# Turning attention weights by DMA: one read instead of four, and more of the query tiles turned that way

## The chip, the cores and the metric

The kernel runs on one core of a Trainium2 chip. The metric is the device time of one execution in microseconds (us), and a kernel's time is the median of its runs. A profile is taken of one execution; its span is the time between the first and the last instruction that the profiler records.

The engines are PE (TensorE, matmuls and transposes through the array; its weight loads are listed apart as PEld), DVE (VectorE), ACT (ScalarE), POOL (GpSimd) and SP (SyncE, which here only issues DMAs). Each works through its own instructions in the order in which they were emitted.

## The reference

One layer of a hybrid trunk, in float32, for a prompt of 1024 rows and a sample group of 32 rows: an RMS norm, one projection to eight parts (q, k, v, g for the head groups A and B), attention in 8 heads of 64 in each group, gates, an output projection, and a gated addition of a second embedding. Only the attention matters here:

```python
def band_attention(q, k, v, q_pos, k_pos, bias_table):          # group A
    s = jnp.einsum('bqhd,bkhd->bhqk', q, k).astype(jnp.float32) * ATTN_SCALE
    s = s + bias_table[:, rel].astype(jnp.float32)[None]
    ...
    w = jax.nn.softmax(s, axis=-1).astype(v.dtype)
    return jnp.einsum('bhqk,bkhd->bqhd', w, v)

def stick_breaking(q, k, v, q_pos, k_pos):                      # group B
    z = jnp.einsum('bqhd,bkhd->bhqk', q, k).astype(jnp.float32) * ATTN_SCALE
    ...
    w = jnp.where(causal, jnp.exp(log_beta + after), 0.0).astype(v.dtype)
    return jnp.einsum('bhqk,bkhd->bqhd', w, v)
```

In A, a query row sees its own chunk of 64 and the eight chunks before; in B it sees all rows before it. The weights `w` have a query row in each partition when they are made, and the product with `v` needs a key in each partition: every tile of weights has to be turned.

## The kernel before, in words

All calls go to a `Recorder` (it stands for `nc`), which notes each instruction with what it reads and writes. At the end a planner (`plan`, line 418, with `due` for due times) runs through all of them with a cost for each, and so settles the order on every engine; `emit` writes the instructions out in that order. In the profile they all have one line, L494, that of `emit`; groups are told apart by the names of their tiles. For PE the order follows a class and the place in the recording: attention has class 0 and is taken when its inputs are ready by the plan, projections have class 1 and fill the rest. All DMAs are issued from SP.

Attention goes by eight pairs of heads, A0, B0, A1, B1 and so on, two heads in each pair. While a pair's attention runs, the projections k, q and v of the next pair (tiles `mm_kA` and so on) are woven in; the last pair has the eight gate projections beside it. A head has eight tiles of 128 query rows, i = 0 to 7. Tile i covers `cost(i)` blocks of 128 keys: in A i + 1 up to 5, in B i + 1 up to 8. For each tile there are two steps:

- `scores(i)`: q times k into PSUM (`SA`, `SB`, each with a high part and a low part of k, `kdA` and `klA`), then, in SBUF, the unnormalised weights. Two tiles are used: `om` (from `ring0`, 3076 columns), which takes the biased scores or the running product, and `be` (from `ring1`, 3328 columns), which takes the weights, by an exponential on ACT in A and by a difference on POOL in B. `rooms(i)` hands out both; the rings are used again from the start when they are full, and a place waits for the last use of what lay there.
- `weights_t(i)`: the turn. It makes `wTh` (a copy of the turned weights, rounded to PE's format) and `wTl` (what the rounding left), one 128x128 block for each block of keys.

The step `values(g)` multiplies them with v for the tiles 0 to 3 (g = 0) and 4 to 7 (g = 1), into `PVA` or `PVB`; it needs the turns of all its tiles. Two tiles lie between the scores of a tile and its turn in the recording (`LAG_T = 2`).

There are two ways to turn a tile. Tiles that do not stand in `ROUND` are turned on PE: a transpose for each block into PSUM (`ptwA`, `ptwB`), up to four blocks in one bank, a copy of the bank by ACT to `wTh`, and a subtraction by DVE that reads the bank and `wTh` and writes `wTl`. Tiles in `ROUND` (4 and 6 of A and of B) go by DMA: DVE transposes all 32x32 squares of `be` into `om` (STREAM_TRANSPOSE `om<-be`), SP issues a write of `om` to a scratch tensor in DRAM (`swapA<-om`, `swapB<-om`), and four reads, each to 32 partitions of `be` (`be<-swapA`, `be<-swapB`), put the squares where they belong. ACT then copies the whole tile to `wTh`, and DVE subtracts from SBUF to get `wTl`. There are four reads because square c of a block holds the columns 32c to 32c + 31, which become the partitions 32c to 32c + 31: each read serves the 32 partitions of one c.

The same way is used for the columns of v in `values_out` (`turn`, once for each of the 8 pairs): `vxA<-stvA` by DVE, a write to `swapA`, four reads into `stvA`; ACT then copies `vtA<-stvA`. The keys (`ktA`, `ktB`) are transposed by DVE alone and written straight out.

Of the kernel before, what the change touches and what calls it, by code (L numbers as in the profile page):

```python
# [13 lines left out]
P = 128  # L14
D = 1024
SEQ = 1024
# [11 lines left out]

ROUND = {"A": ((4,),(6,)), "B": ((4,),(6,))}
LAG_T = 2
LAG_V = 2
SPACE_S = 0.1
# [8 lines left out]
def f(ap):  # L43

    return ap.bitcast(F32)
# [454 lines left out]
def stream_step(  # L500
# [7 lines left out]
    nc = rec  # L508
    dma = nc.sync.dma_start
# [10 lines left out]
    def scratch(shape, name):  # L520
        return Buf(shape, F32, name=name, real=dram.tile(shape, F32, tag=name, name=name))
# [3 lines left out]
    og_dr = scratch([8, P, T], "og_dr")  # L525
    h1_dr = scratch([T, D], "h1_dr")
    sum_dr = {w: scratch([4, 4, P, 512], f"sum_dr{w}") for w in "og"}
    r_dr = scratch([8, 768], "r_dr")
    vs_dr = {ab: scratch([NS, 512], f"vs_dr{ab}") for ab in "AB"}
    ple_dr = scratch([T, D], "ple_dr")  # L530

# [83 lines left out]
    def load_x(t):  # L615
        n = min(P, T - t * P)
        if t == 3:
            x34.append(at.tile([P, ringh.cols], F32, tag="wTh", name="x34")[:, 0:2 * D].rearrange("p (a c) -> p a c", a=2))
        xt = x34[0][:, t - 3] if t in (3, 4) else ring0.tile([P, D], f"x{t}")
        dma(xt[0:n], x_prompt[0, t * P:t * P + n, :] if t < 8 else x_sample[0])  # L620
# [8 lines left out]
    def scale_x(t, xt, n, gp):  # L629
        sq = ring1.tile([P, D], f"sq{t}")  # L630
        ms = small.tile([P, 1], F32, tag="ms", name=f"ms{t}", bufs=4)
        nc.scalar.activation(sq[0:n], xt[0:n], AF.Square, scale=1.0 / 32.0, accum_out=ms[0:n])
        r = rstd_of(ms, f"rs{t}", n)
        for kh in range(2):
            nc.vector.scalar_tensor_tensor(sq[0:n, HALF[kh]], xt[0:n, HALF[kh]], r[0:n], gp[kh][0:n], ALU.mult, ALU.mult)
        return sq
# [68 lines left out]
    def short_block(src, out, nm):  # L705
        pt = psum("T", nm)
        nc.tensor.transpose(pt[0:NS, 0:P], src[:, SEQ:T], ident)
        nc.scalar.copy(out[0:NS, 8, :], pt[0:NS, 0:P])
# [19 lines left out]
    def values_out(ab, p, src, o_p, o_s, then):  # L728

        h2 = slice(2 * p, 2 * p + 2)  # L730
        b0 = 4 if ab == "A" else 0
        box = {}

        def turn():
            st = src()
            D = scratch([P, SEQ], f"swap{ab}{p}")
            x = at2.tile([P, SEQ], F32, tag="tok", name=f"vx{ab}{p}", bufs=2)
            nc.vector.transpose(x.rearrange("p (c b f) -> p b c f", c=4, f=32), st[:, 0:SEQ])
            dma(D, x)
            for c in range(4):  # L740
                part = D[:, c * 256:(c + 1) * 256].rearrange("(g t) x -> t g x", t=32)
                dma(st[32 * c:32 * c + 32, 0:SEQ].rearrange("t (g x) -> t g x", g=4), part)
            out = at2.tile([P, NT, P], F32, tag="tok", name=f"vt{ab}{p}", bufs=2)
            box["out"] = out
            short_block(st, out, f"ptv{ab}{p}")

        def back():
            out = box["out"]
            nc.scalar.copy(out[:, 0:8, :].rearrange("p b (g f) -> p g b f", g=4), src()[:, 0:SEQ].rearrange("p (g b f) -> p g b f", g=4, f=32))
            dma(o_p[0, 0, :, h2, :].rearrange("(b p) h d -> p b (h d)", p=P), out[:, b0:8, :])  # L750
            dma(o_s[0, 0, :, h2, :].rearrange("p h d -> p (h d)"), out[0:NS, 8, :])
            then(out)

        return [(0.1, turn), (0.0, back)]
# [79 lines left out]
    def attention(ab, p, h):  # L834

        nm = f"{ab}{p}{h}"
# [12 lines left out]
        def lo_block(i):  # L849
            return max(0, i - 4) if ab == "A" else 0  # L850

        together = {i: g for g in ROUND[ab] for i in g}
        whole, done_with = {}, []

        def cost(i):
            return i + 1 - lo_block(i)
# [63 lines left out]
        def weights_t(i):  # L920
            g = i // 4
            step, size = LAID[ab, g]
            if g not in wT:
                wT[g] = [x.tile([P, size * P], f"{x.name}{nm}_{g}") for x in (ringh, ringl)]
            b0 = lo_block(i)
            w0, w1 = state.pop(i)
            n = i + 1 - b0
            at_ = ((i - 4 * g) * step + b0) * P
            hi, lo = (x[:, at_:at_ + n * P] for x in wT[g])
            if i in together:  # L930

                group = together[i]
                done_with.append((i, hi, lo))
                if i != group[-1]:
                    return
                w0, w1 = whole[group]
                m = sum(cost(x) for x in group)
                first = {x: sum(cost(y) for y in group[:k]) for k, x in enumerate(group)}
                squares = w0[:, 0:m * P].rearrange("p (c b q) -> p b c q", c=4, q=32)
                for x, _, _ in done_with:  # L940
                    y = slice(first[x], first[x] + cost(x))
                    nc.vector.transpose(squares[:, y], w1[:, y.start * P:y.stop * P])
                dr = scratch([P, m * P], f"swap{nm}_{i}")
                dma(dr, w0[:, 0:m * P])
                for c in range(4):
                    x = dr[:, c * m * 32:(c + 1) * m * 32].rearrange("(g k) x -> k g x", k=32)
                    dma(w1[32 * c:32 * c + 32].rearrange("k (g x) -> k g x", g=4), x)
                turned = w1.rearrange("p (g b q) -> p g b q", g=4, q=32)
                for x, hi, lo in done_with:
                    src = turned[:, :, first[x]:first[x] + cost(x), :]  # L950
                    hi, lo = (y.rearrange("p (b g q) -> p g b q", g=4, q=32) for y in (hi, lo))
                    nc.scalar.copy(hi, src)
                    nc.vector.tensor_tensor(lo, src, f(hi), ALU.subtract)
                done_with.clear()
                return
            for b in range(0, n, 4):
                m = min(4, n - b)
                pt = psum("T", f"ptw{nm}_{i}_{b}")
                for x in range(m):
                    nc.tensor.transpose(pt[:, x * P:(x + 1) * P], w1[:, (b + x) * P:(b + x + 1) * P], ident)  # L960
                c = slice(b * P, (b + m) * P)
                nc.scalar.copy(hi[:, c], pt[:, 0:m * P])
                nc.vector.tensor_tensor(lo[:, c], pt[:, 0:m * P], f(hi[:, c]), ALU.subtract)
# [284 lines left out]
    for n in range(-1, 8):  # L1248
        a = len(order)
        if n < 7:  # L1250
            ab, p = pairs[n + 1]
# [503 lines left out]
    for m, (nm, src, group) in enumerate(sets):  # L1755
        last_set = m == len(sets) - 1
        state = [{}, {}]
        for n, prod in enumerate(ORDER):
            for pair, t in enumerate(group):
                st = state[pair]  # L1760
# [28 lines left out]
                b = blocks[nm, WHICH[prod]]  # L1789
# [70 lines left out]
        if m in (0, 2):  # L1860
            if m == 0:
                row = Row(8, fb.tile([P, D], F32, tag="GP", name="h1_8"))
                row.load()
                for q in range(2):
                    y = short_product(nm, short, q)
# [3 lines left out]
            else:  # L1869
                for q in range(2):  # L1870
                    g8 = Gate(8, HALF[q])
                    y = short_product(nm, short, q)
# [38 lines left out]
```

## Time and profile before

| | |
|---|---|
| runs | 797.0, 799.42, 802.35 us; median 799.42 |
| profiled execution | 796.26 us |
| its span | 794.2 us |
| attention stage, about | 62 to 572 us |
| mean granted clock of TensorE | 0.999 of full speed |
| DMA in all | 161.08 MB, 67.4% of 16 engines' span on the queue that SP issues to |

How to read it: the page gives for each engine its busy time and its share of the span, and forty slices of the span with a digit for the busy tenths in each. The chain is followed back from the last instruction, at each step to what released it. A group of instructions has a line with the output and the input tile, the shapes, the count, the busy time of the group, the mean of one in ns, and the idle time of the engine ahead of them with what ended it. In the list of waits a line has the total, the number of times and the longest, in us. In the chain in order of time a line has the start, the length and what it was; pieces follow one another without overlap.

### The profile page before, as it was taken

The page shows a single profiled execution, that of the slowest core. Times are in us where ns is not written, and L with a number is a line of the kernel's source. Part 1 is how long each engine was busy: PE and PEld are TensorE (multiplying, and loading weights), DVE is VectorE, ACT ScalarE, POOL GpSimd, SP SyncE. Part 2 cuts the span into 40 slices and gives each one's busy share as a digit, 9 for nine tenths or more (in the row PEclk, how much of TensorE's full clock was granted, in tenths as well). Part 3 has the DMA queues.
Part 4 walks back from the last instruction along what each step waited for, and adds up shares of the span by engine and source line. Part 5 has one row for each costly group of instructions (what it writes and reads, how often), then busy time and mean ns, then how long its engine had stood idle before and what let it go on. Part 6 is the DMA issues. An engine that isn't in the chain of part 4 may idle for free.

```text
span 794.2 us, 14262 instructions
## 1 busy us (share of the span) xinstructions
PE 781.9 (98%) x4646; PEld 723.1 (91%) x4646; DVE 572.6 (72%) x1007; ACT 503.8 (63%) x1061; POOL 438.9 (55%) x503
## 2 busy tenths in 40 slices
PE   9999989999999999999999999999999999999997
PEld 7999989999999999999999999999997877888786
DVE  6716868887688889877878788883354878676655
ACT  5636765767686548874677586532348967875741
POOL 5624546874547675424670436787544358597613
PEclk9999999999999999999999999999999999999999
DMA  8519987668887759744544776756489847668634
GB/s 264 170 42 289 229 246 206 180 183 234 233 256 225 206 164 280 194 135 159 132 118 148 169 208 189 234 177 190 126 269 332 282 138 267 225 222 301 232 126 133
DMA packets 160971, 161.08 MB, mean 203 GB/s; under 512 B 39153, under 2 KB 120793, under 8 KB 160898
## 3 DMA queue, kind: packets, MB, share of 16 engines
q1 hardware_dynamic: 160898, 160.18, 67.4%
q8 instruction: 37, 0.61, 0.3%
q14 instruction: 36, 0.29, 0.1%
HBM read 99.23 MB, written 52.49 MB: 191 GB/s over the span
## 4 chain that ended last, share of the span: by engine, by line
PE 91%; DMA 2%; DVE 2%; POOL 2%; issue 1%; ACT 1%; SPq 1%; DVEq 0%; ACTq 0%; POOLq 0%
PE mm_gB L494 6%; PE mm_gA L494 6%; PE mm_qB L494 6%; PE mm_kB L494 6%; PE mm_vA L494 5%; PE mm_kA L494 5%; PE mm_vB L494 5%; PE mm_qA L494 5%; PE PVB L494 4%; PE SB L494 4%; PE SA L494 4%; PE PVA L494 4%; PE ptwB L494 3%; PE g0P L494 2%; PE g1P L494 2%; PE o1P L494 2%
## 5 line engine op out<-in xcount | busy, mean ns | idle before, releaser
L494 POOL TENSOR_TENSOR be<-om 128x384 f32<-128x384 f32 (+7 forms) x64 | 79.0, 1241 | 64.7 <-DVE om L494 38.8
L494 DVE TENSOR_TENSOR_SCAN om<-om,SB 128x384 f32<-128x384 f32 (+5 forms) x96 | 94.2, 999 | 8.7 <-ACT om L494 7.6
L494 ACT ACTIVATE om<-SB 128x384 f32<-128x384 f32 (+5 forms) x96 | 44.4, 492 | 34.0 <-DVE SB L494 23.0
L494 ACT ACTIVATE be<-om,statA 128x640 f32<-128x640 f32 (+4 forms) x64 | 44.5, 696 | 10.1 <-DVE statA L494 6.5
L494 ACT CAST wTh<-ptwB 128x512 fp32r<-128x512 f32 (+3 forms) x64 | 29.4, 481 | 19.5 <-PE ptwB L494 12.2
L494 DVE TENSOR_TENSOR wTl<-ptwB,wTh 128x512 fp32r<-128x512 f32 (+3 forms) x64 | 34.0, 547 | 10.4 <-ACT wTh L494 7.4
L494 DVE TENSOR_TENSOR wTl<-be,wTh 128x640 fp32r<-128x640 f32 (+1 forms) x32 | 35.3, 1105 | 4.7 <-ACT wTh L494 4.3
L494 DVE TENSOR_TENSOR wTl<-ptwA,wTh 128x512 fp32r<-128x512 f32 (+2 forms) x64 | 30.3, 483 | 10.3 <-ACT wTh L494 9.0
L494 DVE CUSTOM_DVE_ANT_0 om<-SA,biasA 128x320 f32<-128x320 f32 (+2 forms) x64 | 29.7, 483 | 9.0 <-PE SA L494 8.3
L494 ACT CAST wTh<-ptwA 128x512 fp32r<-128x512 f32 (+2 forms) x64 | 26.1, 424 | 13.3 <-PE ptwA L494 11.5
L494 DVE STREAM_TRANSPOSE om<-be 128x640 f32<-128x640 f32 (+1 forms) x32 | 29.0, 906 | 6.1 <-POOL be L494 3.5
L494 PE MATMUL SB<-klB,LB 128*128 128x384 f32 (+5 forms) x96 | 33.0, 348 | 0.0
L494 PE MATMUL SB<-kdB,LB 128*128 128x384 f32 (+5 forms) x96 | 32.9, 347 | 0.1
L494 POOL TENSOR_TENSOR oB<-oB,oB 128x256 f32<-128x256 f32 x32 | 24.2, 777 | 13.8 <-DMA oB<-in_w_out_dram 12.5
L494 DVE TENSOR_TENSOR SB<-SB,maskb 128x128 f32<-128x128 f32 x64 | 17.7, 292 | 19.1 <-PE SB L494 19.0
L494 PE MATMUL SA<-klA,LA 128*128 128x320 f32 (+2 forms) x96 | 29.4, 319 | 1.1 <-DMA klA<-klA 1.1
L494 PE MATMUL SA<-kdA,LA 128*128 128x320 f32 (+2 forms) x96 | 30.0, 323 | 0.0
L494 POOL TENSOR_TENSOR gB<-gB,gB 128x256 f32<-128x256 f32 x32 | 26.0, 832 | 6.8 <-DMA gB<-in_w_ple_gate_dram 6.7
L494 PE MATMUL ptwA<-ident,be 128*128 128x128 f32 x160 | 26.2, 273 | 2.7 <-ACT sumrowA L494 2.7
L494 ACT CAST wTh<-be 128x640 fp32r<-128x640 f32 (+1 forms) x32 | 25.0, 781 | 6.1 <-DMA be<-swapA 4.1
L494 PE MATMUL ptwB<-ident,be 128*128 128x128 f32 x192 | 28.7, 273 | 0.0
L494 POOL TENSOR_TENSOR sggA<-sggA,oggA 128x352 f32<-128x352 f32 x24 | 24.9, 1038 | 5.2 <-DMA be<-swapB 2.9
(707 smaller groups left out, 2655.0 us busy)
## 6 DMA issues: line engine op xcount, KB each, us to landing
swapA<-om SPq DMA_DIRECT2D x16, 320.0 KB, 3.6
be<-swapA SPq DMA_DIRECT2D x64, 80.0 KB, 2.8
oB<-in_w_out_dram SPq DMA_DIRECT2D x16, 256.0 KB
sum_dro<-oB SPq DMA_DIRECT2D x16, 256.0 KB, 4.3
gB<-in_w_ple_gate_dram SPq DMA_DIRECT2D x16, 256.0 KB, 4.2
sum_drg<-gB SPq DMA_DIRECT2D x16, 256.0 KB, 2.6
x<-in_x_prompt_dram SPq DMA_DIRECT2D x16, 256.0 KB, 4.1
h_dr<-h SPq DMA_DIRECT2D x8, 512.0 KB, 4.2
```

The lines of the kernel that those rows point to most:

```text
L494: getattr(getattr(tc.nc, o.what[0]), o.what[1])(*args, **kw)
```

## The change

Two edits go together.

The squares that DVE transposes are no longer made of 32 neighbouring columns, but of every fourth column: square c of a block has the columns c, c + 4, c + 8 and so on up to c + 124. After the transpose, the partition 32g + k of `om` holds, for each c, what belongs into the partition 4k + c. Laid out in DRAM as four parts of 128 rows, where row 4k + c of part g is the piece for partition 4k + c, the write is the same as before, and a single read gives each of the 128 partitions its four pieces, one from each part. Four reads of 32 partitions become one of 128; the bytes and the length of a contiguous piece (m x 32 elements, 640 bytes for five blocks) are the same. The input of the DVE transpose is now read with a step of four elements (16 bytes). The value columns get the same edit.

`ROUND` now lists, each by itself, the tiles 4, 5, 6 and 7 of A and 4, 5 and 6 of B. So tiles 5 and 7 of each A head, and tile 5 of each B head, go by DMA and no longer over PE.

```diff
-ROUND = {"A": ((4,),(6,)), "B": ((4,),(6,))}
+ROUND = {"A": ((4,),(5,),(6,),(7,)), "B": ((4,),(5,),(6,))}
...
         def turn():
             st = src()
-            D = scratch([P, SEQ], f"swap{ab}{p}")
+            D = scratch([4, P, SEQ // 4], f"swap{ab}{p}")
             x = at2.tile([P, SEQ], F32, tag="tok", name=f"vx{ab}{p}", bufs=2)
-            nc.vector.transpose(x.rearrange("p (c b f) -> p b c f", c=4, f=32), st[:, 0:SEQ])
-            dma(D, x)
-            for c in range(4):
-                part = D[:, c * 256:(c + 1) * 256].rearrange("(g t) x -> t g x", t=32)
-                dma(st[32 * c:32 * c + 32, 0:SEQ].rearrange("t (g x) -> t g x", g=4), part)
+            nc.vector.transpose(x.rearrange("p (c b f) -> p b c f", c=4, f=32), st[:, 0:SEQ].rearrange("p (b t c) -> p b c t", c=4, t=32))
+            dma(D.rearrange("g (t c) x -> (g t) (c x)", c=4), x)
+            dma(st[:, 0:SEQ].rearrange("p (g x) -> p g x", g=4), D.rearrange("g p x -> p g x"))
...
-                    nc.vector.transpose(squares[:, y], w1[:, y.start * P:y.stop * P])
-                dr = scratch([P, m * P], f"swap{nm}_{i}")
-                dma(dr, w0[:, 0:m * P])
-                for c in range(4):
-                    x = dr[:, c * m * 32:(c + 1) * m * 32].rearrange("(g k) x -> k g x", k=32)
-                    dma(w1[32 * c:32 * c + 32].rearrange("k (g x) -> k g x", g=4), x)
+                    nc.vector.transpose(squares[:, y], w1[:, y.start * P:y.stop * P].rearrange("p (b k c) -> p b c k", c=4, k=32))
+                dr = scratch([4, P, m * 32], f"swap{nm}_{i}")
+                dma(dr.rearrange("g (k c) x -> (g k) (c x)", c=4), w0[:, 0:m * P])
+                dma(w1.rearrange("p (g x) -> p g x", g=4), dr.rearrange("g p x -> p g x"))
```

## The prediction

> **What bounds the kernel now.** I read the page first (busy shares, the 40 slices, the chain), then what PE waited for, then the chain in order of time, and last the groups by form.
>
> ```profile
> span 794.2 us, 14262 instructions
> PE 781.9 (98%) x4646; PEld 723.1 (91%) x4646; DVE 572.6 (72%) x1007; ACT 503.8 (63%) x1061; POOL 438.9 (55%) x503
> DVE  6716868887688889877878788883354878676655
> PE 91%; DMA 2%; DVE 2%; POOL 2%; issue 1%; ACT 1%; SPq 1%; DVEq 0%; ACTq 0%; POOLq 0%
> ```
>
> PE is busy 98% of the span and makes up 91% of the chain that ended last. The next engine, DVE, is at 72%, and of its forty slices of 20 us one reaches 9 (90%). The attention stage runs from about 62 to 572 us; in it PE waited for others three times only:
>
> ```profile
> PE ptwA L494 <- ACT sumrowA L494: 2.7, 1, 2.7
> PE SA L494 <- DMA klA<-klA: 1.1, 1, 1.1
> PE SsB L494 <- DVE QsB L494: 0.5, 1, 0.5
> ```
>
> So in this stage PE is fed all the time: projection matmuls of the next pair fill every hole that attention leaves. Whatever leaves PE shortens the kernel, as long as the fill stays enough and no other engine takes over.
>
> **What leaves PE.** By the code, tiles 5 and 7 of each of A's 8 heads (5 blocks each) and tile 5 of each of B's 8 heads (6 blocks) move from TensorE transposes to the turn by DMA. That is 8 x 10 + 8 x 6 = 128 transposes of the 352 here:
>
> ```profile
> L494 PE MATMUL ptwB<-ident,be 128*128 128x128 f32 x192 | 28.7, 273 | 0.0
> L494 PE MATMUL ptwA<-ident,be 128*128 128x128 f32 x160 | 26.2, 273 | 2.7 <-ACT sumrowA L494 2.7
> ```
>
> The 273 ns are a latency, and matmuls overlap; what one costs the engine is read from the chain in order of time, where each piece begins when the one before ended:
>
> ```profile
> 432.66 0.44 PE ptwA L494 x4
> ...
> 437.44 0.11 PE ptwA L494
> ...
> 454.77 0.55 PE ptwA L494 x5
> ```
>
> 0.11 us each, in groups of one, four and five alike. 128 x 0.11 = 14.1 us less on PE: 20 x 0.11 = 2.2 us for a pair of A heads, 12 x 0.11 = 1.3 us for a pair of B heads. I take 14.1. [...]
>
> **What comes to DVE.** The same tile is turned by one DVE transpose of 32x32 squares, and the low half is then taken from SBUF and not from PSUM. These are the rows, of which the last two give the dearest rate per element that DVE shows:
>
> ```profile
> L494 DVE TENSOR_TENSOR wTl<-be,wTh 128x640 fp32r<-128x640 f32 x24 | 24.3, 1012 | 4.5 <-ACT wTh L494 4.1
> L494 DVE TENSOR_TENSOR wTl<-ptwB,wTh 128x512 fp32r<-128x512 f32 x32 | 21.5, 679 | 7.4 <-ACT wTh L494 4.7 <-PE PVB L494 2.6
> L494 DVE STREAM_TRANSPOSE om<-be 128x640 f32<-128x640 f32 x24 | 20.1, 839 | 6.1 <-POOL be L494 3.5 <-ACT be L494 2.2
> L494 DVE TENSOR_TENSOR wTl<-ptwA,wTh 128x512 fp32r<-128x512 f32 x24 | 16.5, 688 | 6.9 <-ACT wTh L494 6.6
> L494 DVE TENSOR_TENSOR wTl<-be,wTh 128x896 fp32r<-128x896 f32 x8 | 11.1, 1383 | 0.2 <-ACT wTh L494 0.2
> L494 DVE STREAM_TRANSPOSE om<-be 128x896 f32<-128x896 f32 x8 | 8.8, 1105 | 0.1
> L494 DVE TENSOR_TENSOR wTl<-ptwB,wTh 128x256 fp32r<-128x256 f32 x16 | 6.6, 413 | 1.1 <-ACT wTh L494 1.1
> L494 DVE TENSOR_TENSOR wTl<-ptwA,wTh 128x128 fp32r<-128x128 f32 x24 | 6.6, 280 | 1.3 <-ACT wTh L494 1.3
> L494 DVE STREAM_TRANSPOSE ktB<-stkB 128x1024 f32<-128x1024 f32 x4 | 5.0, 1238 | 0.2 <-ACT stkB L494 0.2
> L494 DVE STREAM_TRANSPOSE vxB<-stvB 128x1024 f32<-128x1024 f32 x4 | 4.9, 1231 | 0.0
> ...
> L494 DVE TENSOR_TENSOR_SCAN om<-om,SB 128x512 f32<-128x512 f32 x24 | 30.3, 1262 | 0.8 <-ACT om L494 0.5 <-POOL ksS L494 0.2
> L494 DVE TENSOR_TENSOR_SCAN om<-om,SB 128x384 f32<-128x384 f32 x24 | 23.9, 994 | 1.3 <-ACT om L494 1.2
> ```
>
> A tile of 5 blocks: 839 + 1012 come, 688 + 280 go, +0.88 us. A tile of 6 blocks, midway between the rows of 640 and 896: 972 + 1198 come, 679 + 413 go, +1.08 us. In all 16 x 0.88 + 8 x 1.08 = +22.7 us, off PE's path as long as DVE keeps up. What room DVE has, by stretches (columns: length, then busy time and count of PE, PE's weight loads, DVE, ACT, POOL, then clock, DMA share, GB/s):
>
> ```profile
> 62.00:472.00 410.00, 405.47 (x2627) 392.56 (x2626) 325.95 (x623) 280.24 (x607) 218.23 (x263) 1.00 0.71 200
> 472.00:572.00 100.00, 100.00 (x638) 97.93 (x637) 68.18 (x103) 44.44 (x97) 67.54 (x70) 1.00 0.62 188
> 62.00:112.00 50.00, 46.18 (x304) 44.56 (x302) 36.68 (x82) 33.66 (x75) 23.27 (x29) 1.00 0.95 269
> 300.00:348.00 48.00, 48.00 (x316) 46.49 (x315) 39.75 (x89) 39.66 (x87) 21.83 (x24) 1.00 0.85 229
> ```
>
> The first stretch holds four A pairs and three B pairs. DVE is at 326 of 410 us; with 4 x 3.53 + 3 x 2.16 = 20.6 more it is at 346.6 of the 410 - 12.8 = 397.2 that would be left, 87%. That still fits. The last pair (472 to 572) has 32 us to spare.
>
> **The strided read.** All turns, the 32 that exist, the 24 new ones and the 8 of the value columns, now read every fourth column: a step of 16 bytes from element to element. No row of this trace reads with such a step, so the cost is bounded. From below nothing: the transposes of vxB write runs of 32 scattered over four parts and take 1231 ns, those of ktB write densely and take 1238, so a broken pattern on the write side is free. From above by the dearest rate: a transpose costs (1105 - 839) / 256 = 1.04 ns an element, a scan (1262 - 994) / 128 = 2.09; 1.05 ns more an element is +0.67 us for 640, +0.81 for 768, +0.94 for 896, +1.08 for 1024, together 49.4 us (43.5 of it in the first stretch). I take nothing, since the nearest rows are the transposes themselves, and keep the upper end as a rival. [...]
>
> **ACT, DMA and SP.**
>
> ```profile
> L494 ACT CAST wTh<-be 128x640 fp32r<-128x640 f32 x24 | 17.5, 727 | 4.3 <-DMA be<-swapA 4.1
> L494 ACT CAST wTh<-ptwA 128x512 fp32r<-128x512 f32 x24 | 14.1, 586 | 4.9 <-PE ptwA L494 4.7
> L494 ACT CAST wTh<-ptwA 128x128 fp32r<-128x128 f32 x24 | 6.1, 264 | 3.3 <-PE ptwA L494 3.2
> ```
>
> ACT copies one piece of 640 for two pieces of 512 and 128: 727 - 850 = -0.12 us a tile, some 3 us less in all: no change. POOL does no other work, though the low halves from SBUF may make it wait.
>
> ```profile
> swapA<-om SPq DMA_DIRECT2D x16, 320.0 KB, 3.6
> be<-swapA SPq DMA_DIRECT2D x64, 80.0 KB, 2.8
> ```
>
> ```profile
> L494 SPq DMA_DIRECT2D be<-swapA x64: 302/432/866, 84.0 to 467.6; - x64
> ```
>
> Before, a turn costs five issues on SP; after, two. The 32 existing turns and the 8 value turns drop 3 x 40 = 120 issues, the 24 new ones add 48: 72 fewer, x 0.43 = 31 us less on SP's queue. The one read of 320 KB should land like the write of 320 KB, 3.6 us, against 3 x 0.43 + 2.8 = 4.1 for the last of four: at worst 0.8 us later than a single part is now, at best half a microsecond sooner; taken as equal. But SP waits in order, and a read stands there until its write has landed, with every later issue behind it:
>
> ```profile
> SPq L494 <- DMA swapB<-om: 9.0, 6, 2.2
> ```
>
> That is 9.0 us over 16 turns, 0.56 each; 24 more make 13.5 us of SP's time, under the 31 us that it gains. The new turns move 16 x 2 x 320 + 8 x 2 x 384 KB, 16.8 MB more, about a tenth on top of 161 MB. DMA has room but for the first pair, at 0.95 from 62 to 112 us, where PE already loses 3.8 us. There SP's queue held back a chain:
>
> ```profile
> 108.06 3.93 SPq L494 DMA_DIRECT2D be<-swapA  x8
> ...
> 111.22 0.26 ACT L494 COPY sumrowA<-ptsA 8x128 f32<-8x128 f32 x1 [3.66 <-DMA o_dr<-otA]
> ```
>
> Eight reads would be two (and two more for the new tiles). That could give back up to the 2.7 us of PE's longest wait, and the crowded DMA could take as much; I set the two against each other, nothing.
>
> **The wait that is new.** In A, tile 7 is the last before the value product of tiles 4 to 7, which PE can't begin before its turn is back. Tile 6 is turned that way already:
>
> ```profile
> 432.07 0.84 DVE L494 STREAM_TRANSPOSE om<-be 128x640 f32<-128x640 f32 x1
> ...
> 440.67 0.59 ACT L494 CAST wTh<-ptwA 128x512 fp32r<-128x512 f32 x1 [0.71 <-PE ptwA L494]
> ...
> 445.74 0.82 DVE L494 TENSOR_TENSOR wTl<-be,wTh 128x640 fp32r<-128x640 f32 x1
> ```
>
> Fifteen microseconds lie between tile 6's turn and the product, which begins at 447.13, and PE filled them with projections. Tile 7 comes behind it through the same queues: one DVE transpose 0.84, an issue 0.43 + 0.35, a copy 0.73 and a low half 0.82, 3.2 us later. The cover is the projection work of the next pair, 35 us a pair (216 matmuls at 0.16). I cost it at nothing; without cover it is 3.2 x 8 = 25 us. In B tile 6 is already late and tile 7 stays on PE, so tile 5 adds no wait at the end.
>
> **Sum.** 794.2 - 14.1 = 780.1 us of span; the profiled execution took 796.26, so 782.2. The median of the runs, 799.42, is 3.2 above the profiled one: 785.4, said as 786.
>
> **Rivals.**
> 1. DVE takes over (the other side). If the step of 16 bytes doubles the transposes' rate, the first stretch has 346.6 + 43.5 = 390.1 us of DVE work in 397.2, 98%, and only one slice of forty reaches 90% now. If DVE sustains 94%, the stretch lasts 415.0, 17.8 us more than PE needs: 782.2 + 17.8 = 800.0, on the median's scale 803, slower than before. At 90% it is 433, 821; if DVE can be filled wholly, it is 786. At 94% it decides from a step cost of 38.8 us in the stretch: about nine tenths of the doubling. For it: no row shows the step free. Against it: DVE's waits, such as 19 us for PE SB, shrink when it is late.
> 2. Tile 7's turn makes PE wait: up to 25 us, 811; it beats the saving from 14.1 / 8 = 1.8 us a head. Against it: of PE's three waits in the stage, which has 32 such turns in it, none was for a turn.
> 3. The gain is eaten by small losses (first pair's crowded DMA, POOL held by the SBUF low halves, the rings of score tiles held longer, an order of the queues that suits less): half or two thirds lost, 793 to 796. Here too belongs that the one read lands later than four.
>
> **How the numbers follow.** Forecast with what is near it 0.47, rival 1 0.29, rival 2 0.11, rival 3 0.13. About 1% (8 us) is what can be told from no change: faster is below 791.4, slower above 807.4. The forecast gives faster in nearly nine of ten of its cases, rival 1 is mostly within 1% and slower in a third, rival 2 is slower in two of three, rival 3 is within. Faster 0.46, same 0.32, slower 0.22. The range: 779 (the 2.7 us wait and the spread of the runs below) to 809, which leaves out the harder half of rivals 1 and 2; the forecast's own is 780 to 792.
>
> **What would show it.** Right: ptwA x80 and ptwB x144; PE busy near 768 us; STREAM_TRANSPOSE om<-be 128x640 x40 still near 840 ns; DVE near 595 us; be<-swap x56. Wrong: that row near 1500 ns with PE waiting for DVE; PE waiting for wTl before PVA; be<-swap landing far over 4 us.

## The result, and the profile after

The changed kernel takes 796.43 us, the median of 12 runs (792.05 to 800.34), beside 799.61 us for the kernel before in the same session (12 runs, 797.0 to 802.35). The ratio is 0.9959, with a 95% interval of 0.9939 to 0.9978: 3.3 us faster (1.8 to 4.9), where 13.4 were forecast. In what follows, a per cent of the time is 8.0 us, and each kernel is given by its ratio to the kernel before in its own session.

The profiled execution of the changed kernel took 797.65 us, 1.2 above its median; that of the kernel before took 796.26, 3.3 below its own. The two spans (795.9 and 794.2 us) therefore stand the wrong way round, and the reading goes by busy times and waits. The page after:

```profile
span 795.9 us, 13838 instructions
PE 775.4 (97%) x4518; PEld 710.2 (89%) x4518; DVE 622.2 (78%) x1007; ACT 502.9 (63%) x1039; POOL 438.3 (55%) x503
DVE  6716799899899789999899799986446778676655
```

PE makes 128 matmuls fewer (4646 to 4518), as it should. Its busy time fell by 6.5 us and not by 14, and DVE's rose by 49.6 us and not by 22.7. What PE waited for between 62 and 600 us, where only three waits stood before:

```profile
PE PVB L494 <- ACT wTh L494: 2.4, 3, 1.1
PE SB L494 <- DVE om L494: 2.2, 4, 0.9
PE ptksB L494 <- DMA be<-in_cache_b_k_dram: 1.0, 1, 1.0
PE PVA L494 <- ACT wTh L494: 1.0, 1, 1.0
PE PVB L494 <- DVE v2B L494: 0.8, 1, 0.8
PE ptsA L494 <- DVE sumsA L494: 0.8, 2, 0.6
```

The list goes on with five more of 0.3 to 0.8 us: many small waits on ACT, DVE, POOL and DMA, and the one big wait (2.7 us for `sumrowA`) is all but gone. The first rows are products that wait for the copy of a turned tile, and scores that wait for DVE to free their bank. One such wait in the chain of the changed kernel, in order of time (start, length, what):

```profile
382.99 0.69 DVE SB L494 x3
383.69 0.06 SPq L494
383.75 0.05 issue
383.80 6.33 DMA be<-swapB
390.13 0.02 issue
390.15 0.95 ACT wTh L494
391.10 0.04 issue
391.14 1.20 PE PVB L494 x4
```

SP, which waits in order, is released by DVE at 383.69 us and comes to the read of a turned tile; 6.33 us pass before its data lets ACT go on, ACT copies, and only then does PE begin the value product, after 1.07 us of waiting.

How much of the stage PE is idle is read from one stretch that holds nearly all of it, in the kernel before and then after (length, then busy time and count of PE, PE's weight loads, DVE, ACT, POOL, then clock, DMA share, GB/s):

```profile
62.00:597.00 535.00, 530.47 (x3420) 515.43 (x3418) 405.32 (x743) 334.95 (x723) 297.41 (x343) 1.00 0.70 200
```

```profile
62.00:597.00 535.00, 522.83 (x3288) 501.49 (x3287) 454.77 (x743) 334.60 (x700) 296.81 (x344) 1.00 0.77 230
```

PE's idle time grew from 4.5 to 12.2 us. The transposes that are left and the operations of the turns, by group and form:

```profile
L494 PE MATMUL ptwB<-ident,be 128*128 128x128 f32 x144 | 22.0, 273 | 1.0 <-POOL be L494 0.8 <-POOL oB L494 0.2
L494 PE MATMUL ptwA<-ident,be 128*128 128x128 f32 x80 | 12.8, 274 | 0.3 <-ACT sumrowA L494 0.2
```

```profile
L494 DVE STREAM_TRANSPOSE om<-be 128x640 f32<-128x640 f32 x40 | 52.7, 1329 | 0.9 <-ACT be L494 0.4 <-POOL be L494 0.3
L494 DVE TENSOR_TENSOR wTl<-be,wTh 128x640 fp32r<-128x640 f32 x40 | 38.7, 975 | 3.1 <-ACT wTh L494 3.0
L494 DVE STREAM_TRANSPOSE om<-be 128x896 f32<-128x896 f32 x8 | 14.5, 1809 | 1.8 <-POOL be L494 1.8
L494 DVE STREAM_TRANSPOSE om<-be 128x768 f32<-128x768 f32 x8 | 12.6, 1573 | 1.1 <-POOL be L494 1.0
...
L494 DVE STREAM_TRANSPOSE vxB<-stvB 128x1024 f32<-128x1024 f32 x4 | 8.2, 2047 | 0.9 <-ACT stvB L494 0.9
...
L494 DVE STREAM_TRANSPOSE ktB<-stkB 128x1024 f32<-128x1024 f32 x4 | 5.0, 1239 | 0.0
```

The counts are those of the diff. The step of 16 bytes is not free: (1809 - 1329) / 256 = 1.88 ns an element instead of 1.04, while `ktB`, read densely, stays at 1239 ns.

### The profile page after: what moved, and what is told of

It reads as the page before. It is cut to its first block, busy times and chain, and to the rows that moved or that the text cites. A ratio compares the mean times of both kernels' runs of the same rounds, so it can differ in the third digit from the quotient of the medians.

```text
span 795.9 us, 13838 instructions
## 1 busy us (share of the span) xinstructions
PE 775.4 (97%) x4518; PEld 710.2 (89%) x4518; DVE 622.2 (78%) x1007; ACT 502.9 (63%) x1039; POOL 438.3 (55%) x503
## 4 chain that ended last, share of the span: by engine, by line
PE 41%; DVE 8%; issue 2%; DMA 2%; ACT 1%; POOL 0%; SPq 0%; DVEq 0%; ACTq 0%; POOLq 0%
PE mm_gB L494 6%; PE mm_gA L494 4%; DVE om L494 3%; PE g0P L494 2%; PE o1P L494 2%; PE g1P L494 2%; PE g2P L494 2%; PE o0P L494 2%; PE g3P L494 2%; PE o3P L494 2%; PE o2P L494 2%; PE ple L494 2%; PE PVB L494 2%; PE mm_vA L494 1%; DVE wTl L494 1%
## 5 line engine op out<-in xcount | busy, mean ns | idle before, releaser
L494 DVE STREAM_TRANSPOSE om<-be 128x640 f32<-128x640 f32 (+2 forms) x56 | 79.8, 1433 | 3.8 <-POOL be L494 3.2
L494 DVE TENSOR_TENSOR wTl<-be,wTh 128x640 fp32r<-128x640 f32 (+2 forms) x56 | 58.6, 1050 | 10.3 <-ACT wTh L494 10.1
L494 ACT CAST wTh<-be 128x640 fp32r<-128x640 f32 (+2 forms) x56 | 43.1, 771 | 17.7 <-DMA be<-swapB 12.5
L494 DVE CUSTOM_DVE_ANT_0 om<-SA,biasA 128x320 f32<-128x320 f32 (+3 forms) x64 | 29.8, 482 | 6.8 <-PE SA L494 4.8
L494 ACT CAST wTh<-ptwB 128x512 fp32r<-128x512 f32 (+3 forms) x48 | 22.3, 483 | 17.7 <-PE ptwB L494 11.2
L494 POOL TENSOR_TENSOR klB<-stkB,kdB 64x1024 fp32r<-64x1024 f32 x8 | 20.4, 2548 | 13.7 <-ACT kdB L494 9.3
L494 DVE TENSOR_TENSOR wTl<-ptwB,wTh 128x512 fp32r<-128x512 f32 (+3 forms) x48 | 25.4, 542 | 3.1 <-ACT wTh L494 1.6
L494 PE MATMUL PVB<-wTh,v2B 128*128 128x512 f32 (+1 forms) x96 | 22.2, 354 | 3.2 <-ACT wTh L494 2.4
L494 POOL TENSOR_TENSOR h<-h,x 128x512 f32<-128x512 f32 (+1 forms) x18 | 23.9, 1350 | 0.0
L494 PEld LDWEIGHTS PVB<-wTh,v2B 128*128 128x128 f32 x96 | 17.6, 193 | 7.1 <-ACT wTh L494 3.3
L494 POOL TENSOR_TENSOR klA<-stkA,kdA 64x1024 fp32r<-64x1024 f32 x8 | 19.5, 2438 | 7.6 <-ACT kdA L494 7.4
```

The source lines that it names most:

```text
L494: getattr(getattr(tc.nc, o.what[0]), o.what[1])(*args, **kw)
```

## The experiments

Three readings of the missing 10 us were open. DVE: the step of 16 bytes and the rest of DVE's new work hold PE up. The turn: tiles come back late, through a longer DMA path. PE's own queue: it was not the only thing that set the pace, so that work taken from it comes back as waits, whoever takes it over. Beside these stood a fourth, that the planner's new order is simply a worse one. Where an edit changes what is recorded, the planner lays out a new order for it, and the time then holds the worth of both; the text says so where the order was held. A landing constant of the planner is named below: it is the time (2.5 us) by which the planner takes a transfer's data to be there after its line.

### The step of 16 bytes: taken to ACT, taken to ACT and POOL

Here the writer of `be` puts the columns where DVE can read them densely, and itself writes with a step of 128 bytes: ACT's exponential for A alone, then ACT for A and POOL's difference for B. The value columns keep the step on DVE. The order of the instructions on every engine is that of the changed kernel.

```diff
+                out, src = w1[:, 0:n], w0[:, 0:n]
+                if i in together:
+                    out = out.rearrange("p (b c k) -> p b k c", c=4, k=32)
+                    src = src.rearrange("p (b k c) -> p b k c", c=4, k=32)
-                nc.scalar.activation(w1[:, 0:n], w0[:, 0:n], AF.Exp,
+                nc.scalar.activation(out, src, AF.Exp,
...
-                    nc.vector.transpose(squares[:, y], w1[:, ...].rearrange("p (b k c) -> p b c k", c=4, k=32))
+                    nc.vector.transpose(squares[:, y], w1[:, ...])
```

> The changed kernel, but in A the order of every fourth column is made by ACT when it writes the weights (the exponential of the 32 DMA-turned tiles writes with a step of 128 bytes), so that DVE's transposes in A read densely again; B and the value columns stay as in the change. DVE loses 32 x 0.49 = 15.7 us, ACT gets at most 32 x 0.83 = 27 us more (63% busy now). If the time is set by SP's issues and DVE's load together: 788 to 793. If DVE's load doesn't count and only the order and SP's queue do: 794 to 800.

> As the run before, and in B POOL writes the weights in that order (24 tiles, step of 128 bytes), so that of DVE's transposes only the 8 of the value columns keep the step. DVE loses some 30 us against the changed kernel and stands near 592 us, like the kernel with four reads; SP has as few issues as the change. If both counted: 784 to 790. If DVE's load doesn't count: 794 to 800. A slower POOL (up to 36 us more) would show as PE waiting for be.

A alone: 798.46 us, ratio 0.9970 (0.9949 to 0.9991). A and B: 796.70 us, ratio 0.9957 (0.9935 to 0.9978), the same as the changed kernel's 0.9959. With A and B, DVE's busy time fell from 622.2 to 598.6 us and its transposes of the weights were as fast as before the change, while PE's waits were about as long (11.1 us idle between 62 and 597 us):

```profile
L494 DVE STREAM_TRANSPOSE om<-be 128x640 f32<-128x640 f32 x40 | 32.6, 825 | 5.5 <-ACT be L494 4.8 <-POOL be L494 0.7
```

```profile
PE ptsA L494 <- DVE sumsA L494: 2.5, 4, 1.0
PE SB L494 <- DVE om L494: 1.9, 3, 0.9
PE ptosA L494 <- ACT be L494: 1.7, 1, 1.7
PE PVB L494 <- ACT wTh L494: 1.1, 1, 1.1
```

So the step costs DVE 24 to 30 us that set nothing here: in the same order and without it the kernel is as fast. (With the old list, below, it is not free.) ACT paid for the step in A (its exponential of 640 went from 831 to 1493 ns), so a step that is free for everybody was not tried.

### The parts of the change, one without the other

The new list with the old squares and four reads, and the old list with the new squares and one read, each in an order of its own:

```diff
 # e1: the kernel before, and
-ROUND = {"A": ((4,),(6,)), "B": ((4,),(6,))}
+ROUND = {"A": ((4,),(5,),(6,),(7,)), "B": ((4,),(5,),(6,))}
 # e2: the changed kernel, and
-ROUND = {"A": ((4,),(5,),(6,),(7,)), "B": ((4,),(5,),(6,))}
+ROUND = {"A": ((4,),(6,)), "B": ((4,),(6,))}
```

> The changed list of tiles (4 to 7 of A, 4 to 6 of B) with the old squares and the four reads, so that no DVE read has a step. Theory 1 (the step of 16 bytes costs DVE some 36 us, and PE waits for DVE): the 128x640 transposes are back near 840 ns, DVE near 590 us, and the time is 785 to 790 us, 6 to 11 below the changed kernel. Theory 2 (the new turns themselves, their wait ahead of the value product and the fuller DMA queues, eat the gain): 794 to 800, as the changed kernel or worse, since SP issues 72 reads more for the new tiles.

> The old list of tiles (4 and 6) with the new squares and the single read. Theory 1: 32 + 8 transposes cost about 25 us more of DVE and nothing leaves PE, so it is no faster than before: 799 to 804. Theory 2: the shorter queue of SP helps, or at least does no harm: 796 to 799.

The list alone is slower, and more so than either theory had it: 812.94 us, ratio 1.0153 (1.0123 to 1.0182). The single read alone gains nothing: 800.99 us, 1.0019 (1.0001 to 1.0036). With four reads SP issued 650 DMAs between 62 and 572 us and spent 349 us on it, against 550 and 275 before and 476 and 260 in the changed kernel. Turned tiles came late to ACT, which waited 12.7 us for those of A alone:

```profile
L494 ACT CAST wTh<-be 128x640 fp32r<-128x640 f32 x40 | 29.2, 730 | 16.8 <-DMA be<-swapA 12.7 <-DMA be<-swapB 3.8
```

The same row of the changed kernel:

```profile
L494 ACT CAST wTh<-be 128x640 fp32r<-128x640 f32 x40 | 28.9, 726 | 6.7 <-DMA be<-swapB 3.4 <-DMA be<-swapA 2.8
```

The two edits belong together, as far as two orders can show it: with the single read the longer list goes from 1.0153 to 0.9959. Then the old list, one read, and the step on ACT and POOL; and the changed kernel without tile 7 of A:

```diff
 # e7: as with the step on ACT and POOL, and
-ROUND = {"A": ((4,),(5,),(6,),(7,)), "B": ((4,),(5,),(6,))}
+ROUND = {"A": ((4,),(6,)), "B": ((4,),(6,))}
 # e8: the changed kernel, and
-ROUND = {"A": ((4,),(5,),(6,),(7,)), "B": ((4,),(5,),(6,))}
+ROUND = {"A": ((4,),(5,),(6,)), "B": ((4,),(5,),(6,))}
```

> The old list of tiles, the single read, the order made by ACT and POOL: against the kernel before, 120 issues fewer on SP and DVE's load as it was. It shows what the shorter queue is worth alone. If SP's queue held PE back in the kernel before: 793 to 797. If not, since PE was busy 98%: 798 to 801.

> The changed kernel with tile 7 of A back on PE (tiles 4 to 6 in both groups): PE gets 40 x 0.11 = 4.4 us back, DVE loses 8 x (1.33 + 0.98 - 0.68 - 0.28) = 10.8 us, SP 16 issues. If the turn of tile 7 ahead of the value product is what eats the gain: 786 to 792. If it is DVE's load: 793 to 798. If PE's own work decides: 800.

Without any new tile: 798.79 us, 0.9983 (0.9966 to 0.9999), so a shorter SP queue by itself, in the order that the planner made for it, is worth about 1.4 us. Its order is that of the old list with the step on DVE (1.0019), on every engine: there moving the step off DVE is worth 2.9 us (1.0 to 4.8), so it is not free in every kernel. Without tile 7: 803.13 us, 1.0030 (1.0007 to 1.0053), slower than with it, in another order. A wait for tile 7 is not what eats the gain: in all of the changed kernel PE waited 1.0 us for ACT's copies ahead of `PVA`, by the list of waits above.

### Low halves on POOL, and a planner that knows the step

```diff
 # e4
-                    nc.vector.tensor_tensor(lo, src, f(hi), ALU.subtract)
+                    (nc.gpsimd if x in (5, 7) else nc.vector).tensor_tensor(lo, src, f(hi), ALU.subtract)
 # e3, in the planner's costs for DVE
+            if method == "transpose" and len(args[1].shape) == 4:
+                return 130 + 1.88 * n, 85
```

> The changed kernel, with the low half of the turned tiles 5 and 7 subtracted by POOL and not by DVE: about 26 us of DVE work less (16 of 0.98, 8 of 1.17), and some 36 us more for POOL, which is at 55%. Theory 1: 788 to 792, since DVE is what is short. Theory 2: no change or slower, 796 to 802, since the wait of tile 7 grows by POOL's longer instruction.

> The changed kernel, with the planner told the measured cost of a transpose with the step (130 + 1.88 ns an element in place of 100 + 1.04). No work differs, only the order. Theory 1 as lack of DVE time: within 2 us of the changed kernel (794 to 798). Theory 3 (the order was laid out for transposes that are too short, so PE's instructions stand ahead of data that comes late): 786 to 792.

Both are slower, and above every range that was expected: 805.33 us (1.0064, 1.0039 to 1.0089) and 805.96 us (1.0077, 1.0054 to 1.0100). With 24 of the low halves on POOL, DVE's busy time hardly fell (620.6 us): those of 640 that stayed on DVE took 1398 ns in the mean, where all 40 took 975. By the means of the changed kernel the 24 that left took 16 x 0.975 + 8 x 1.171 = 25.0 us, and the 24 longer ones add 24 x 0.423 = 10.2, which makes 607.4 us of 622.2; so some 13 us more, by estimate, lie in other work of DVE. That POOL's low halves did this is not shown (see the last section). And a truer cost in the planner, which leaves all work as it is, made the order worse by 1.2%. That was the first sign that the order by itself moves the time by more than the change does.

### PE's queue by itself

These two leave all other engines, all DMAs and the order as they are, and change PE's work alone, by 128 transposes. In the kernel before 128 are left out (only the last of each group of four, or of two, is made, and the copies read its block several times); in the changed kernel 128 are made twice.

```diff
 # e13: the kernel before, and
+                few = i in ((3, 5, 7) if ab == "A" else (3, 5))
                 for x in range(m):
                     nc.tensor.transpose(pt[:, x * P:(x + 1) * P], w1[:, (b + x) * P:(b + x + 1) * P], ident)
+                    rec.ops[-1].skip = few and x < m - 1
...
 # e12: the changed kernel, and
                     nc.tensor.transpose(pt[:, x * P:(x + 1) * P], w1[:, (b + x) * P:(b + x + 1) * P], ident)
+                    rec.ops[-1].again = i in (0, 2, 3)
```

> The kernel before with the same order of instructions on every engine, but 128 of PE's transposes left out (in query tiles 3, 5, 7 of A's heads and 3, 5 of B's, only the last transpose of each group is made, and the copies read its block for all), so part of the attention weights is not computed. No DVE, ACT, POOL or DMA work is added. Theory A (the PE term was right, and the change's own costs ate the rest): 799.6 - 14.1 = 785.5 us (784 to 787.5). Theory C (without the transposes PE runs into the other engines at once, whoever takes them away): 790 to 795 us, with new waits of PE on DVE, ACT and DMA.

> The changed kernel with the same order of instructions on every engine, but the 128 transposes of query tiles 0, 2 and 3 of both kinds of head are made twice on PE into the same place: nothing else is added. If PE is as tight as the 97% says and a transpose is worth 0.11 us, 128 of them give back the 14.1 us: 796.4 + 14.1 = 810.5 us (809 to 812). If PE's new waits have left it slack in which added work hides, a good part is swallowed: 801 to 807 us.

Without 128 transposes: 795.62 us, ratio 0.9929 (0.9905 to 0.9954), 5.7 us faster (3.7 to 7.6) and not 14.1. With 128 more: 803.95 us, 1.0041 (1.0026 to 1.0056), 6.6 us more than the changed kernel and not 14.1. Both ways a transpose is worth 0.04 to 0.05 us of the kernel's time and not 0.11.

The transposes do cost PE what was said. From start to start in the timeline of PE, the `ptwA` and `ptwB` between 62 us and the last `mm_gB` took 33.8 us before and 21.1 us with 128 fewer of them, 0.10 us each. But in the same stretch the projection matmuls of 128x352, 2097 in both, went from 349.6 to 357.0 us, waits included, and all other matmuls from 151.1 to 155.0. So of the 12.7 us between these two executions 11.3 came back as waits and slower matmuls; their times (796.26 and 794.96 us) differ by 1.3 us, where the ratio says 5.7, since the profiled execution of the kernel before is 3.3 us below its median. The busy times with 128 left out, PE's stretch from 62 to 597 us, and the longest of its waits (`emit` has line 501 here):

```profile
PE 773.3 (98%) x4518; PEld 709.6 (90%) x4518; DVE 570.8 (72%) x1007; ACT 503.3 (63%) x1061; POOL 440.6 (56%) x503
62.00:597.00 535.00, 523.84 (x3297) 503.79 (x3297) 404.38 (x745) 335.85 (x726) 299.11 (x343) 1.00 0.71 200
```

```profile
PE ptwA L501 <- ACT sumrowA L501: 4.3, 2, 3.5
PE PVsA L501 <- ACT newh L501: 1.6, 1, 1.6
PE PVsA L501 <- DVE otA L501: 1.2, 1, 1.2
PE PVA L501 <- ACT wTh L501: 1.0, 1, 1.0
PE SA L501 <- DMA klA<-klA: 0.9, 2, 0.5
PE PVB L501 <- ACT wTh L501: 0.7, 2, 0.5
```

PE's idle time is 11.2 us against 4.5 before, though DVE, ACT, POOL and the DMAs have not a single instruction more. That is nearly as much as the changed kernel shows (12.2 us). So a gain of this size goes missing without any new turn. It does not go in the same places: 7.1 of the 11.2 us are waits for `sumrowA` and ahead of the products `PVsA`, for which PE waits 0.2 us in the changed kernel. That both kernels lose the rest of the gain for the same reason is therefore not shown. Nor was an order tried that the planner makes for fewer transposes without new turns.

### A quarter of the bytes

The turns keep their issues, and each engine its order, but the turns of weight tiles move a quarter of their bytes; first in the changed kernel, then in the kernel before, then in the kernel before less 128 transposes.

```diff
                 dma(dr.rearrange("g (k c) x -> (g k) (c x)", c=4), w0[:, 0:m * P])
+                rec.ops[-1].part = lambda ap: ap[0:32]
                 dma(w1.rearrange("p (g x) -> p g x", g=4), dr.rearrange("g p x -> p g x"))
+                rec.ops[-1].part = lambda ap: ap[:, 0:1]
```

> The changed kernel with the same order of instructions on every engine, but each turned tile's write and read move only a quarter of their bytes (32 partitions out, one of the four parts back), so three quarters of each turned weight tile is left out of the computation. Theory A (PE's new waits come from turned tiles that land late, and from transfers that crowd): the write and the read are each about 1 us shorter, some 2 us a turn, the ACT copies stop waiting for swapA and swapB, and about half of the 11 us that came back goes: 788 to 792 us. Theory B (the bytes don't matter: the order of issue on SP and the order on ACT and DVE set it): 795.5 to 797.5 us, with PE's waits as in the changed kernel.

> The kernel before with the same order of instructions on every engine, but its turns move a quarter of their bytes (32 partitions out, one of four parts in each of the four reads), so part of the turned weights is left out. If the 7 us that quartering gave the changed kernel (790.7 beside its 797.6 on that scale) is a cost of the change's own 16.8 MB more, the kernel before gains little from it: 797 to 800 us. If late turns are a common tail of both kernels, it gains as much: 791 to 795 us.

> The kernel before less 128 of PE's transposes (795.6 us before, where 14.1 us came off PE's queue and 5.2 off the time), with its turns moving a quarter of their bytes; the order on every engine is that of the kernel before. If what PE runs into, once its queue is shorter, is the landing of turns, most of the lost 9 us comes back: 785 to 789 us. If it is the order and load of ACT, DVE and SP, 792 to 795.5 us.

Changed kernel: 790.71 us, 0.9871 (0.9852 to 0.9891), 7.0 us better than with all bytes. Kernel before: 797.65 us, 0.9964 (0.9939 to 0.9988), 2.9 us better. Less 128 transposes: 789.25 us, 0.9863 (0.9831 to 0.9895), 5.3 us better than with all bytes. So bytes matter in all three. Of the 8.4 us that were missing with 128 transposes left out, 5.3 come back, or 2.4 beyond what the kernel before gains from the same cut; each gain is uncertain by 2 to 3 us, so that bytes matter more where PE is shorter is not shown by these two. The rest is not the bytes of the turns. In the profile of this last kernel PE's idle time in the stretch is 8.0 us, between the 11.2 and the 4.5:

```profile
62.00:597.00 535.00, 527.02 (x3324) 508.02 (x3323) 410.50 (x751) 341.32 (x738) 301.14 (x344) 1.00 0.62 171
```

### The order

Last, the landing constant of the planner, which changes no work at all:

```diff
-DMA_RATE, LANDING, WAKE_DMA = 320.0, 2500, 200
+DMA_RATE, LANDING, WAKE_DMA = 320.0, 4000, 200    # 1500, 2400
```

> The changed kernel with one constant of its planner raised: a transfer is taken to land 4.0 us after its line instead of 2.5 us, nearer to the 5.5 to 6.0 us that the trace shows from one step of a turn to the next. The work is the same, only the order differs. Theory A (engines stand in order behind turns that land later than planned): 788 to 793 us. Theory B (one order is about as good as another, the rest is chance): 793 to 803 us, either side of 796.4 us.

> The changed kernel with the planner's landing constant lowered from 2.5 to 1.5 us; same work, another order. The raised constant (4.0 us) cost it 20 us. If the time falls steadily with the constant, because whatever is planned early keeps PE fed, 785 to 792 us; if the order as it stands is near the best and each departure from it costs, 799 to 815 us.

> The kernel before with the planner's landing constant lowered from 2.5 to 1.5 us; same work, another order: the control to the one above. If a shorter landing helps whatever the kernel, 789 to 796 us. If each departure from the order as it stands costs, 802 to 815 us. The spread over these orders says how much of a difference of 3 us between two kernels can be the luck of their orders.

> The changed kernel with the planner's landing constant moved by a twenty-fifth, from 2.5 to 2.4 us: the work is the same, the order of issue differs in many places. If the order as it stands is neither lucky nor unlucky, 795 to 798 us on the scale where the changed kernel stands at 796.4; if the orders scatter, up to 8 us to either side. A time under 794 would be a version that beats both kernels.

> The kernel before with the same nudge, 2.5 to 2.4 us. If the order as it stands is neither lucky nor unlucky, 798 to 801 us; if the orders scatter, up to 8 us to either side. Beside the nudged changed kernel it says whether the change's 3.2 us survive another pair of orders (796 and 799.5 would be the same gain again).

| landing constant | kernel before | changed kernel |
|---|---|---|
| 1.5 us | 817.78 us, 1.0209 (1.0171 to 1.0248) | 806.96 us, 1.0095 (1.0061 to 1.0128) |
| 2.4 us | 807.83 us, 1.0089 (1.0063 to 1.0114) | 809.35 us, 1.0101 (1.0082 to 1.0120) |
| 2.5 us | 1 | 796.43 us, 0.9959 (0.9939 to 0.9978) |
| 4.0 us | not tried | 817.87 us, 1.0221 (1.0199 to 1.0244) |

A nudge of 0.1 us costs the kernel before 7.1 us (0.9%) and the changed one 11 us (1.4%). In that pair of orders the changed kernel is not faster than the one before (1.0101 and 1.0089, intervals overlapping); at 1.5 us it is faster by 1.1%. The 0.4% of the result is the difference between two particular orders. It is real for these two kernels, but the runs do not show that the change is worth it whatever the order. Every other constant that was tried made its kernel slower, by 0.9 to 2.6%.

This bears on the experiments above. The step on ACT and POOL, the transposes left out or made twice and the quarter of the bytes hold the order of their kernel. The lists, the low halves on POOL and the planner's cost do not, and their differences of 0.2 to 1.5% from the kernel before are no larger than what an order does. Seven runs came out 2.8 us or more above all that was expected of them (four reads, low halves on POOL, the planner's cost, no tile 7, 4.0 us, the kernel before at 1.5 us, and the changed kernel at 2.4 us), and each of them has a new order.

No version was found that beats the changed kernel: the one with the step on ACT and POOL ties with it, and the faster ones leave work out.

## Why the prediction was wrong, point by point

**The step that failed** is the first: "So in this stage PE is fed all the time", and from it "Whatever leaves PE shortens the kernel, as long as the fill stays enough and no other engine takes over". PE was fed, but only just: no engine took over when its queue became shorter (DVE stands at 72% before and with 128 transposes left out), and yet what was priced at 14.1 us gave 5.7 us (3.7 to 7.6) when nothing else was touched. Three waits in 510 us were read as a margin. They showed only that at the speed PE then had, in an execution 3.3 us faster than the median, its inputs came in time; they did not say by how much. Work put on PE was swallowed to half in the same way (6.6 us showed of 14.1), which the 98% does not let one expect.

**What leaves PE** was right as an amount: 128 transposes, and 0.10 us each from start to start where they were left out. By that rate the 14.1 us are 12.7. It was wrong as a term of the sum, taken in full, where 5.7 us came.

**What comes to DVE** was right without the step: with the new list and the old squares DVE's busy time is 593.1 us, 20.5 more than before, where 22.7 were worked out. **The strided read**, "I take nothing", measured 40 x 0.49 + 8 x 0.60 + 8 x 0.70 + 8 x 0.81 = 36.5 us of DVE time, three quarters of the upper bound, at 1.88 against 1.04 ns an element by the rows of 640 and 896; the row nearest to the new operation misled. Yet this error did not make the time. Rival 1, with DVE filled to 94%, needed nine tenths of the upper bound; DVE was at 365.6 of 410 us (89%) in its first stretch, and the kernel in the same order without the step on the weights is as fast.

```profile
62.00:472.00 410.00, 399.17 (x2513) 381.04 (x2512) 365.61 (x615) 276.58 (x579) 215.39 (x258) 1.00 0.78 230
```

**ACT** was right (502.9 us against 503.8). **SP**: in the stretch from 62 to 572 us the issues of the turns went from 200 to 128 and their time from 91.0 to 60.8 us, close to the 31 us worked out. But SP's other issues, 350 and 348 of them, grew from 183.9 to 199.0 us, and took half of it back; in the same order with a quarter of the turns' bytes they take 178.0 us, so the turns' bytes made these issues longer. A single read takes 0.50 us to issue in the median in A and 0.42 in B, against 0.43 for each of the four:

```profile
L494 SPq DMA_DIRECT2D be<-swapA x32: 365/504/1835, 84.2 to 480.2; - x32
```

**DMA**: 177.8 MB against 161.1, as worked out. The single read landed in 3.6 us, like the write, where a trace shows its landing (three of the 16 reads with the old list); the changed kernel's trace shows none:

```profile
be<-swapA SPq DMA_DIRECT2D x16, 320.0 KB, 3.6
```

The two effects of which it says "I set the two against each other, nothing" were of unlike size. SP's relief alone is worth about 1.4 us in its order, and the cut of the bytes is worth 4.1 us (uncertain by 3) more to the changed kernel than to the one before. **Tile 7's wait** was rightly costed at nothing, and rival 2 falls: PE's waits for copies ahead of `PVA` are 1.0 us in all, where it had up to 25.

**The rivals.** The outcome lies beside the 793 to 796 of rival 3, whose mechanism is half right: the crowded DMA is in it, but its picture was a gain of 14 us eaten by the change's own losses, and with only PE's queue cut most of it does not come either. From the kernel less 128 transposes (0.9929) to the changed kernel (0.9959) there are 2.4 us (uncertain by 2.5) of own costs less own gains, not 11. What this 2.4 is made of stays open: it is far below what another order of the same work does.

Open too is which of ACT, DVE, SP and the landings PE meets first once it is shorter. The runs show that the bytes of the turns are a part, and that in this order the step on DVE is none.

## What to carry to other kernels

Here PE, at 98% and with few waits, was the bound only for the next few microseconds (5.7 of the 14.1 us priced): before pricing work taken from such an engine at its full duration, find out how early its inputs arrive, or leave a little of its work out with everything else held, which here gave 40% of the price. In a kernel with a fixed order on every engine, compare a change that is worth 1% or less in more than one order, because moving one constant of the planner by 4% made the two kernels 0.9 and 1.4% slower. A duration that no row shows deserves the middle of its bounds and not its lower end, but a longer duration on an engine with slack still has to be shown to be a longer time.

## What the runs showed of the hardware

**PE's clock fell to about half after some of its waits.** In the kernel less 128 transposes PE waited 3.5 us for `sumrowA`; for the next 4 us its clock was about half, 0.54 and 0.61 (stretches of 2 us: length, PE's busy time and count, granted clock, DMA share, GB/s):

```profile
108.00:110.00 2.00, 0.49 (x4) 1.00 0.79 250
110.00:112.00 2.00, 0.00 (x0) 1.00 0.83 234
112.00:114.00 2.00, 1.99 (x7) 0.54 0.76 196
114.00:116.00 2.00, 2.00 (x9) 0.61 0.75 209
116.00:118.00 2.00, 2.00 (x14) 1.00 1.02 317
```

The kernel before waits at the same place for 2.7 us, with some PE work between, and keeps its clock:

```profile
108.00:110.00 2.00, 0.80 (x7) 1.00 0.76 226
110.00:112.00 2.00, 0.48 (x5) 1.00 0.87 252
112.00:114.00 2.00, 2.00 (x15) 1.00 0.73 198
```

Laid beside that of the kernel before, PE's timeline falls back by another 1.0 us from 112.2 to 116.0 us. But the changed kernel falls to about half (0.57 and 0.58), too, where no single wait was over 0.94 us: four waits lie between 272.6 and 276.5 us, with five matmuls among them, so one long wait was not needed there. What lowered the clock is not shown.

```profile
276.00:278.00 2.00, 1.52 (x4) 0.57 1.10 337
278.00:280.00 2.00, 2.00 (x11) 0.58 0.53 172
```

The mean granted clock of all runs was 0.990 with the new list and four reads and 0.990 with the planner that knows the step, against 0.997 for the kernel before and after the change. Over a span of 800 us that is 5 to 6 us by estimate, of the 9.4 us by which the second of them is slower than the changed kernel, and of the 12.2 us by which the first is slower than the kernel before.

**The step had a price on each engine, and not the same.** DVE's transpose of 640 went from 839 to 1329 ns reading with a step of 16 bytes. ACT's exponential of 640, writing with a step of 128 bytes, went from 831 to 1493 ns. POOL's difference went with the same step from 1408 to 1548 ns for 640, from 1687 to 1726 for 768 and from 1769 to 1980 for 896.

**DVE's subtraction of 640 from SBUF took over 881 ns only beside POOL.** In the traces of all the kernels here, 219 low halves of 640 (`wTl<-be,wTh`) overlap no instruction of POOL in time, and they took 761 to 881 ns. The 429 that overlap one took 770 to 4053 ns, 1211 in the mean. DVE's dense transposes of 640 took 0.83 us with POOL beside them and without (88 of them, in three kernels). So the mean of this group hung on what POOL did at its side, and that need not be low halves. Here are the means with 24 of the low halves on POOL, and with the old list and one read, where POOL has none:

```profile
L494 DVE TENSOR_TENSOR wTl<-be,wTh 128x640 fp32r<-128x640 f32 x24 | 33.5, 1398 | 5.1 <-ACT wTh L494 4.1 <-issue 1.0
L494 DVE TENSOR_TENSOR wTl<-be,wTh 128x640 fp32r<-128x640 f32 x24 | 32.6, 1358 | 3.2 <-ACT wTh L494 3.2
```
